# Input projection weights kept as split pairs in DRAM, and attention rows scaled on VectorE

## The chip, the cores and the metric

The kernel runs on one core of a Trainium2 chip. The metric is the device time of one execution in microseconds; the kernel before took 3005.1 us (median of 3 runs, 3004.28 to 3007.91). The profiled execution is one separate run.

## The reference

One decoder layer over 2048 tokens with 1024 features, all in fp32:

```
u = rmsnorm(h, attn_norm_g);  z = u @ w_in            # 1024 x 3592, the input projection
y_m = mLSTM of 4 heads from the columns (q, k, v, output gate, input and forget gate)
y_a = differential attention of 4 heads: two softmax maps of 64 dims per head, (A1 - lam A2) v
o   = rmsnorm(o, sub_g) * (1 - lam_init)               # per head and row, the end of y_a
h  += concat(y_m, y_a) @ w_out
h  += square(relu(rmsnorm(h) @ w_up)) @ w_down         # 1024 -> 4096 -> 1024
h  += sigmoid(rmsnorm(h) @ w_gate) * (p @ w_ple)
```

## The kernel before

**Split operands.** Every large product runs in a rounded fp32 type (F32R). To keep fp32 accuracy each operand x is split: hi is x rounded (a copy on ScalarE, line 75) and lo is x minus hi (a subtraction on GpSimd or VectorE, line 76). A product is three matmuls, hi·hi, hi·lo and lo·hi (`mm3`, lines 134 to 139).

**Two parts.** The first part (`phase1`) computes the input projection, mLSTM, attention and the first eighth of the output projection; the second (`phase2`, whose matmuls are line 923) the rest. The change is in the first part, which in the trace ends near 1290 us, where the first matmul of line 923 stands.

**Stages.** The tokens are cut into 4 tiles of 512, and the input projection's columns into 14 groups, 0 to 7 for mLSTM and 8 to 13 for attention. `ORDER` (line 37) gives eight stages: attention columns of tiles 0, 1, 2, mLSTM columns of tiles 0 and 1, attention of tile 3, mLSTM of tiles 2 and 3. Counted by the 192 matmuls of line 137 in each, the stages begin on TensorE at 6, 112, 243, 372, 525, 702, 839 and 1017 us, and the first out-projection at 1221 us. An attention stage uses 6 groups, an mLSTM stage 8, and each stage loads and splits its own weights, though other stages use the same ones for other tokens.

**Weights.** `load_w` (line 242) brings one group in four pieces of two 128-row blocks: SyncE issues a load into one of two `wraw` buffers (tile `rbuf` in the profile), ScalarE and GpSimd split it into one of eight hi and eight lo buffers (tile `wbuf`). `next_w` (line 265) calls it for the next group when the current one is about to be used, so loads run one group ahead. That makes 24 pieces in an attention stage, 32 in an mLSTM stage, 224 in all.

**Interleaving.** Attention units (one head, 128 query rows) run beside the projection. A loop in `phase1` (lines 575 to 593) picks the next piece of either by costs written in the code; mLSTM steps are woven in between. The order of instructions on each engine is then set at build time by a scheduler with its own timeline, so every engine works through a fixed list and waits at its head.

**Where the attention rows are scaled.** `attn_back` (line 815) sums the squares of the head's output on ScalarE (line 840), forms the argument on VectorE (841, 842), takes the power -1/2 on GpSimd (843) and multiplies the 128x128 tile by it on GpSimd (844). TensorE transposes the result (line 500) one unit later. The same pattern stands in `qk_prep` (line 723): a power on GpSimd (734), then products on VectorE (736).

**Queues.** All the DMAs of the kernel are issued by SyncE, in order, from one list.

Of the kernel before, what the change touches and what calls it, by code (L numbers as in the profile page):

```python
# [7 lines left out]
F32 = mybir.dt.float32  # L8
F32R = mybir.dt.float32r
BF16 = mybir.dt.bfloat16  # L10
AF = mybir.ActivationFunctionType
ALU = mybir.AluOpType
# [4 lines left out]
P = 128  # L17
D = 1024
S = 2048
KT = D // P  # L20
# [9 lines left out]
NW, NR, NKT, LEAD = 8, 2, 4, 4  # L30
# [10 lines left out]
def hybrid_block(ctx: ExitStack, tc: tile.TileContext, a: dict, out: bass.AP):  # L41
    nc = tc.nc

    const = ctx.enter_context(tc.tile_pool(name="const", bufs=1))
    dram = ctx.enter_context(tc.tile_pool(name="dram", bufs=1, space=DRAM))
# [7 lines left out]
    vdr = dram.tile([NH // 2, NT1, P, 4, 2 * P], F32, name="v_d")  # L53

# [40 lines left out]
    phase1(tc, a, wbuf, ubuf, rbuf, banks, yT, hd, qkdr, vdr, ident, identr, identb, masks, ones, negh, split, rstd_col, spread, acc0)  # L95
# [80 lines left out]
def phase1(tc, a, wbuf, ubuf, rbuf, ps, yT, hd, qkdr, vdr, ident, identr, identb, masks, ones, negh, split, rstd_col, spread, acc0):  # L176
    nc = tc.nc
    with ExitStack() as ctx:
# [7 lines left out]
        half = NW * 528  # L186
        for tag, base in (("whi", 0), ("wlo", half)):
            pw.put(tag, [cut(wbuf, base + i * 528, 2, 264) for i in range(NW)])
# [53 lines left out]
        def load_w(g, width, first=False):  # L242
            r = []
            for k in range(0, KT, 2):
                raw = pw.tile([P, 2, 264], F32, tag="wraw")[:, :, :width]
                hi = pw.tile([P, 2, 264], F32R, tag="whi")
                lo = pw.tile([P, 2, 264], F32R, tag="wlo")
                nc.sync.dma_start(raw, w_in[g, :, k:k + 2, :width])
                hi, lo = hi[:, :, :width], lo[:, :, :width]
                if first and k % 4 == 0:  # L250
                    nc.vector.tensor_copy(hi, raw)
                    nc.vector.tensor_tensor(out=lo, in0=raw, in1=hi.bitcast(F32), op=ALU.subtract)  # L252
                else:
                    split(raw, hi, lo)
                r += [(hi[:, i], lo[:, i]) for i in range(2)]
            return r

        wseq, wq = [], []
        for kind, j in ORDER:
            if kind == "a":  # L260
                wseq += [(8, 264)] + [(8 + g, 256) for g in range(1, 6)]
            else:
                wseq += [(g, 256) for g in (0, 1, 2, 3, 4, 5, 7, 6)]
# [551 lines left out]
def attn_back(nc, pa, ps, st, i, h, front, VV, ident, negh, out):  # L815
# [28 lines left out]
    nc.gpsimd.tensor_scalar(out=y, in0=y, scalar1=ss[:, 0:1], scalar2=None, op0=ALU.mult)  # L844
# [378 lines left out]
```

## Time and profile before

| | |
|---|---|
| median of 3 runs | 3005.1 us (3004.28 to 3007.91) |
| profiled execution | 2999.47 us, span 2997.7 us |
| mean granted TensorE clock | 0.988 of full speed |
| TensorE busy | 2872.7 us, 96% of the span |
| VectorE, ScalarE, GpSimd busy | 66%, 46%, 42% |
| DMA | 282.57 MB, 94 GB/s |

The page gives busy times over the whole span; the first part has other limits than the second, so it is read in windows. A window's PEclk is the mean clock that was granted, as a share of full speed. The durations of matmuls overlap, because they are pipelined. "Idle before" is the time an engine stood still before an instruction, with what released it.

### The profile page before, as it was taken

Reading aid. Unit: us, or ns where it says so; the run is one execution under the profiler, and the core shown is the slowest. Engines: PE = TensorE matmul, PEld = TensorE weight load, DVE = VectorE, ACT = ScalarE, POOL = GpSimd, SP = SyncE. Lnnn points to the kernel's source line nnn. Section 1 sums busy time; section 2 is a strip of 40 time slices with the busy share of each in tenths; the row PEclk is TensorE's granted clock in tenths of the full one; section 3 lists DMA queues with packets and bytes.
Section 4 is the critical chain, followed back from the end, with each engine's and each line's share of the span. In section 5 each row is a group of like instructions: output and inputs, shape, how many; then the busy total and the mean of one; then the engine's idle time right before and its main releaser. Section 6 shows DMA issues by size and latency. Waiting matters only on the chain.

```text
span 2997.7 us, 43151 instructions
## 1 busy us (share of the span) xinstructions
PE 2872.7 (96%) x15752; PEld 2460.7 (82%) x15752; DVE 1963.7 (66%) x3917; ACT 1377.7 (46%) x3134; POOL 1267.0 (42%) x980
## 2 busy tenths in 40 slices
PE   7798999899999899989999999999999999999999
PEld 7787988888988788867888888888878888888887
DVE  7788777767786766567555656564486555565653
ACT  4476766766666665544223332252342233322331
POOL 5666543434443332344333333362563333333441
PEclk9899999999999999999999999999999999999999
DMA  5654544334443423341111111124411111111211
GB/s 160 193 159 146 175 135 123 110 103 138 140 128 96 123 81 100 105 163 49 51 57 43 57 57 50 53 75 154 134 60 53 57 43 57 57 50 50 80 48 64
DMA packets 202421, 282.57 MB, mean 94 GB/s; under 512 B 16096, under 2 KB 143584, under 8 KB 198112
## 3 DMA queue, kind: packets, MB, share of 16 engines
q1 hardware_dynamic: 202208, 279.81, 30.7%
q8 instruction: 124, 2.03, 0.3%
q14 instruction: 89, 0.73, 0.1%
HBM read 239.90 MB, written 39.85 MB: 93 GB/s over the span
## 4 chain that ended last, share of the span: by engine, by line
PE 69%; DVE 14%; ACT 5%; DMA 4%; issue 4%; POOL 3%; SPq 0%; POOLq 0%; ACTq 0%; DVEq 0%
PE bank L923 52%; PE bank L137 3%; PE bank L138 3%; PE bank L139 3%; PE bank L834 2%; DMA rbuf<-in_w_in_dram 2%; DVE qn_r L736 2%; POOL wbuf L76 2%; DVE PP_r L810 2%; ACT PP_r L798 1%; DVE mxp_r L790 1%; PE bank L786 1%; PE bank L789 1%; PE bank L822 1%; POOL rn_r L734 1%
## 5 line engine op out<-in xcount | busy, mean ns | idle before, releaser
L76 POOL TENSOR_TENSOR wbuf<-rbuf,wbuf 128x512 fp32r<-128x512 f32 (+2 forms) x632 | 911.8, 1450 | 1321.8 <-ACT wbuf L75 1230.0
L75 ACT ACTIVATE wbuf<-rbuf 128x512 fp32r<-128x512 f32 (+2 forms) x632 | 415.1, 662 | 870.2 <-PE bank L923 600.7
L923 PE MATMUL bank<-U_r,wbuf 128*128 128x512 f32 x2928 | 701.1, 392 | 10.3 <-POOL wbuf L76 4.7
L923 PEld LDWEIGHTS bank<-U_r,wbuf 128*128 128x128 f32 x2928 | 551.1, 189 | 129.9 <-POOL wbuf L76 6.1
L923 PE MATMUL bank<-ubuf,wbuf 128*128 128x512 f32 x2208 | 574.7, 391 | 2.2 <-DVE ubuf L76 1.4
L888 DVE TENSOR_TENSOR h_r<-bank,h_r 128x512 f32<-128x512 f32 x504 | 343.3, 688 | 269.1 <-PE bank L923 267.5
L923 PEld LDWEIGHTS bank<-ubuf,wbuf 128*128 128x128 f32 x2208 | 414.8, 188 | 92.7 <-issue 2.9
L923 PE MATMUL bank<-ybuf,wbuf 128*128 128x512 f32 x1872 | 477.5, 390 | 5.4 <-ACT wbuf L75 4.6
L923 PEld LDWEIGHTS bank<-ybuf,wbuf 128*128 128x128 f32 x1872 | 351.3, 188 | 80.2 <-ACT wbuf L75 5.9
L137 PE MATMUL bank<-wbuf,ubuf 128*128 128x256 f32 (+1 forms) x1280 | 381.1, 298 | 25.0 <-ACT og_r L397 10.1
L138 PE MATMUL bank<-wbuf,ubuf 128*128 128x256 f32 (+1 forms) x1280 | 375.4, 293 | 0.9 <-DVE wbuf L252 0.9
L139 PE MATMUL bank<-wbuf,ubuf 128*128 128x256 f32 (+1 forms) x1280 | 373.6, 292 | 0.6 <-DVE ubuf L76 0.6
L137 PEld LDWEIGHTS bank<-wbuf,ubuf 128*128 128x128 f32 x1280 | 250.4, 196 | 34.1 <-ACT og_r L397 12.6
L138 PEld LDWEIGHTS bank<-wbuf,ubuf 128*128 128x128 f32 x1280 | 251.1, 196 | 3.9 <-DVE wbuf L252 1.5
L139 PEld LDWEIGHTS bank<-wbuf,ubuf 128*128 128x128 f32 x1280 | 250.5, 196 | 2.8 <-DVE ubuf L76 0.7
L790 DVE TENSOR_REDUCE mxp_r<-bank 128x1 f32<-128x512 f32 (+3 forms) x320 | 186.3, 603 | 68.6 <-PE bank L789 68.1
L798 ACT ACTIVATE PP_r<-bank,mx_r 128x512 f32<-128x512 f32 (+3 forms) x320 | 196.3, 622 | 53.8 <-DVE mx_r L795 47.4
L834 PE MATMUL bank<-V_r,at_r 128*128 128x128 f32 x1088 | 137.8, 279 | 0.9 <-ACT at_r L825 0.5
L786 PE MATMUL bank<-KT_r,QT_r 128*128 128x512 f32 (+3 forms) x320 | 124.7, 390 | 12.8 <-ACT PP_r L798 10.9
L834 PEld LDWEIGHTS bank<-V_r,at_r 128*128 128x128 f32 x1088 | 132.3, 196 | 3.4 <-ACT at_r L825 0.8
L137 PE MATMUL bank<-ubuf,wbuf 128*128 128x512 f32 x320 | 130.2, 407 | 2.4 <-DVE mx_r L794 1.2
L139 PE MATMUL bank<-ubuf,wbuf 128*128 128x512 f32 x320 | 127.8, 399 | 0.0
(285 smaller groups left out, 4244.8 us busy)
## 6 DMA issues: line engine op xcount, KB each, us to landing
rbuf<-in_w_in_dram SPq DMA_DIRECT2D x208, 256.0 KB, 2.8
rbuf<-in_w_down_dram SPq DMA_DIRECT2D x128, 256.0 KB, 2.6
rbuf<-in_w_up_dram SPq DMA_DIRECT2D x32, 1024.0 KB, 4.8
KT_r<-qk_d SPq DMA_DIRECT2D x40, 512.0 KB, 5.0
qk_d<-kst_r SPq DMA_DIRECT2D x64, 256.0 KB, 3.1
QT_r<-qk_d SPq DMA_DIRECT2D x128, 128.0 KB, 3.4
rbuf<-in_w_out_dram SPq DMA_DIRECT2D x32, 512.0 KB, 3.8
rbuf<-in_x_in_dram SPq DMA_DIRECT2D x31, 512.0 KB, 3.8
```

The lines of the kernel that those rows point to most:

```text
L75: nc.scalar.activation(hi, raw, AF.Copy)
L76: eng.tensor_tensor(out=lo, in0=raw, in1=hi.bitcast(F32), op=ALU.subtract)
L137: nc.tensor.matmul(ps, lhsT=lh, rhs=rh, start=(start and i == 0), stop=False)
L138: nc.tensor.matmul(ps, lhsT=lh, rhs=rl, start=False, stop=False)
L139: nc.tensor.matmul(ps, lhsT=ll, rhs=rh, start=False, stop=(stop and i == n - 1))
L736: nc.vector.scalar_tensor_tensor(out=qn[:, e], in0=qn[:, e], scalar=rn[:, e:e + 1], in1=qkg[:, e // 2], op0=ALU.mult, op1=ALU.mult)
L786: nc.tensor.matmul(Sp[:, 0:n], lhsT=QT[:, 0, m], rhs=rhs, start=True, stop=False)
L790: nc.vector.tensor_reduce(out=mxp[:, m, ci:ci + 1], in_=Sp[:, 0:n], op=ALU.max, axis=AX.X)
L798: nc.scalar.activation(pp[:, 0:n], sps[ci][:, 0:n], AF.Exp, bias=mx[:, m:m + 1], scale=0.125, accum_out=lp[:, m, ci:ci + 1])
L834: nc.tensor.matmul(po, lhsT=ats[kb // 4][:, (kb % 4) * P:(kb % 4 + 1) * P], rhs=VV[kb // 4][:, kb % 4], start=(kb == 0), stop=(kb == i))
L888: eng.tensor_tensor(out=out, in0=x, in1=y, op=op)
L923: nc.tensor.matmul(p, lhsT=l, rhs=r, start=start and i == q == 0, stop=stop and i == n - 1 and q == 2, skip_group_check=on)
```

## The change

Both parts of a split weight piece now lie side by side in one buffer `ws` (hi first, lo second). In the first stage that uses a group for keeping, the pieces are loaded and split as before, and each pair is then stored to a DRAM tensor `wsd`; the store is put into the program two pieces later. Attention groups 8 to 10 are kept in tile 1's stage (tile 0's stage splits them and does not store), groups 11 to 13 in tile 0's stage, mLSTM groups in tile 0's stage: 56 stores of 512 KB. In later stages the piece is one load of 512 KB from `wsd` straight into `ws`, without a split: 156 of the 224 pieces. In `attn_back` the multiplication of the tile moves from GpSimd to VectorE.

```
+    wsd = dram.tile([14, KT // 2, P, 4, 264], F32, name="ws_d")
...
-        half = NW * 528
-        for tag, base in (("whi", 0), ("wlo", half)):
-            pw.put(tag, [cut(wbuf, base + i * 528, 2, 264) for i in range(NW)])
+        pw.put("ws", [cut(wbuf, i * 1056, 2, 2, 264) for i in range(NW)])
...
+        kept, late_st = set(), []
+        flat4 = lambda t: t.bitcast(F32).rearrange("p a b c -> p (a b) c")
+        def store_w(lag):
+            while len(late_st) > lag:
+                ws, g, k, n = late_st.pop(0)
+                nc.sync.dma_start(wsd[g, k // 2, :, :, :n], flat4(ws)[:, :, :n])
-        def load_w(g, width, first=False):
+        def load_w(g, width, keep, first=False):
             r = []
             for k in range(0, KT, 2):
+                ws = pw.tile([P, 2, 2, 264], F32R, tag="ws")
+                hi, lo = ws[:, 0, :, :width], ws[:, 1, :, :width]
+                if g in kept:
+                    store_w(0)
+                    nc.sync.dma_start(flat4(ws)[:, :, :width], wsd[g, k // 2, :, :, :width])
+                    r += [(hi[:, i], lo[:, i]) for i in range(2)]
+                    continue
                 raw = pw.tile([P, 2, 264], F32, tag="wraw")[:, :, :width]
...
                     split(raw, hi, lo)
                 r += [(hi[:, i], lo[:, i]) for i in range(2)]
+                if keep:
+                    late_st.append((ws, g, k, width))
+                store_w(2)
+            if keep:
+                kept.add(g)
...
-                wseq += [(8, 264)] + [(8 + g, 256) for g in range(1, 6)]
+                wseq += [(8 + g, 256 if g else 264, j == (0 if g >= 3 else 1)) for g in range(6)]
             else:
-                wseq += [(g, 256) for g in (0, 1, 2, 3, 4, 5, 7, 6)]
+                wseq += [(g, 256, j == 0) for g in (0, 1, 2, 3, 4, 5, 7, 6)]
...
-    nc.gpsimd.tensor_scalar(out=y, in0=y, scalar1=ss[:, 0:1], scalar2=None, op0=ALU.mult)
+    nc.vector.tensor_scalar(out=y, in0=y, scalar1=ss[:, 0:1], scalar2=None, op0=ALU.mult)
```

In the order of instructions three places show it. The line numbers of the changed kernel are larger by 1 up to the head of `phase1`, and by 17 behind `load_w`.

GpSimd's list at the end of the last mLSTM stage, up to the first weights of the output projection (128x1024), before. Line 76 is the subtraction of a split, 706 and 843 are powers, 844 the scaling of an attention tile:

```order
L706 TENSOR_TENSOR mss_r<-mss_r,negh 128x4
L76 TENSOR_TENSOR wbuf<-rbuf,wbuf 128x2x256 x4
L843 TENSOR_TENSOR ass_r<-ass_r,negh 128x1
L844 TENSOR_SCALAR ya_r<-ya_r,ass_r 128x128
L76 TENSOR_TENSOR wbuf<-rbuf,wbuf 128x2x256 x4
L843 TENSOR_TENSOR ass_r<-ass_r,negh 128x1
L844 TENSOR_SCALAR ya_r<-ya_r,ass_r 128x128
L706 TENSOR_TENSOR mss_r<-mss_r,negh 128x4
L76 TENSOR_TENSOR wbuf<-rbuf,wbuf 128x2x256 x4
L843 TENSOR_TENSOR ass_r<-ass_r,negh 128x1
L844 TENSOR_SCALAR ya_r<-ya_r,ass_r 128x128
L76 TENSOR_TENSOR wbuf<-rbuf,wbuf 128x1024
```

The same place of GpSimd's list now (706 is 723, 843 is 860, 76 is 77):

```order
L723 TENSOR_TENSOR mss_r<-mss_r,negh 128x4
L860 TENSOR_TENSOR ass_r<-ass_r,negh 128x1 x2
L723 TENSOR_TENSOR mss_r<-mss_r,negh 128x4
L860 TENSOR_TENSOR ass_r<-ass_r,negh 128x1
L723 TENSOR_TENSOR mss_r<-mss_r,negh 128x4
L860 TENSOR_TENSOR ass_r<-ass_r,negh 128x1 x3
L723 TENSOR_TENSOR mss_r<-mss_r,negh 128x4
L77 TENSOR_TENSOR wbuf<-rbuf,wbuf 128x1024 x2
```

Only the powers are left; the splits of the weights and the scaling are gone from this stretch.

SyncE's list where the mLSTM columns of tile 1 end and the attention columns of tile 3 begin (128x528 is the first group), before. Line 248 loads a raw weight piece, 464, 441 keys and queries of attention, 719 stores an mLSTM result:

```order
L248 DMA rbuf<-in_w_in_dram 128x2x256 x4
L464 DMA KT_r<-qk_d 128x1024 x2
L248 DMA rbuf<-in_w_in_dram 128x2x256 x2
L441 DMA QT_r<-qk_d 64x2x256 x4
L248 DMA rbuf<-in_w_in_dram 128x2x256 x2
L464 DMA KT_r<-qk_d 128x1024
L719 DMA yT_d_74<-yo_r 128x512
L997 DMA pre<-yT_d_74 128x512
L248 DMA rbuf<-in_w_in_dram 128x2x256 x6
L248 DMA rbuf<-in_w_in_dram 128x528 x2
L441 DMA QT_r<-qk_d 64x2x256 x4
```

The same place now (257 loads a split pair, 481 and 458 are keys and queries, 736 is the store):

```order
L257 DMA wbuf<-ws_d 128x4x256 x4
L481 DMA KT_r<-qk_d 128x1024 x2
L458 DMA QT_r<-qk_d 64x2x256 x4
L481 DMA KT_r<-qk_d 128x1024
L736 DMA yT_d_74<-yo_r 128x512
L1014 DMA pre<-yT_d_74 128x512
L257 DMA wbuf<-ws_d 128x4x256 x8
L458 DMA QT_r<-qk_d 64x2x256 x4
L257 DMA wbuf<-ws_d 128x1056
```

A group's four loads now stand in one run, and each waits for TensorE to let go of its buffer instead of for the split of the raw buffer.

VectorE's list at one attention unit of the last mLSTM stage, now. Line 859 is before's 842, 861 the scaling that came from GpSimd's line 844:

```order
L859 SCALAR_TENSOR_TENSOR ass_r<-ass_r 128x1
L811 TENSOR_REDUCE mx_r<-mxp_r 128x1
L812 TENSOR_SCALAR mx_r<-mx_r 128x1
L712 SCALAR_TENSOR_TENSOR C_1_125<-C_1_125,g_ct_r,bank_72 128x129
L713 TENSOR_TENSOR N_r<-bank_72,I_r 128x129
L861 TENSOR_SCALAR ya_r<-ya_r,ass_r 128x128
L696 SCALAR_TENSOR_TENSOR Dm_r<-bank_73,Dm_r 128x128
```

Between 859 and 861, which waits for GpSimd's power of 859's result, four other instructions stand here; over the 64 units it is 0 to 16, and in 15 of them at most one.

## Rows read from the trace of the kernel before

**Rows 1.** Section 1 of the page: engine, busy us, share, instructions.
```profile
PE 2872.7 (96%) x15752; PEld 2460.7 (82%) x15752; DVE 1963.7 (66%) x3917; ACT 1377.7 (46%) x3134; POOL 1267.0 (42%) x980
```

**Rows 2.** Busy time by stage: window, length, engines with instruction counts, clock, DMA share, GB/s.
```profile
core 0: us, PE busy (x) PEld busy (x) DVE busy (x) ACT busy (x) POOL busy (x), PEclk, DMA share, GB/s
0.00:112.00 112.00, 87.45 (x646) 83.13 (x647) 83.17 (x247) 51.36 (x96) 63.87 (x56) 0.98 0.60 172
112.00:166.00 54.00, 43.46 (x296) 40.13 (x295) 44.96 (x157) 28.51 (x72) 35.34 (x36) 0.85 0.55 166
166.00:355.00 189.00, 173.45 (x1360) 161.46 (x1359) 156.35 (x535) 129.67 (x366) 113.24 (x112) 0.98 0.54 157
355.00:502.00 147.00, 143.41 (x989) 128.64 (x989) 116.59 (x301) 99.17 (x279) 69.62 (x59) 1.00 0.47 139
502.00:702.00 200.00, 189.33 (x1323) 171.36 (x1322) 147.41 (x355) 137.79 (x394) 80.28 (x68) 0.99 0.39 115
702.00:839.00 137.00, 126.99 (x993) 119.61 (x992) 101.23 (x309) 92.16 (x247) 66.44 (x63) 0.98 0.49 145
839.00:1017.00 178.00, 169.83 (x1125) 149.86 (x1124) 135.07 (x303) 116.52 (x323) 67.71 (x54) 0.98 0.35 103
1017.00:1221.00 204.00, 189.94 (x1285) 168.69 (x1286) 134.54 (x327) 130.15 (x375) 57.47 (x50) 0.98 0.33 96
```

**Rows 3.** Chain of waits by line: 166:355, then 702:839, then 1017:1221.
```profile
by line: DVE qn_r L736 10.7%; issue 9.6%; DVE mxp_r L790 5.4%; POOL wbuf L76 5.2%; PE bank L137 4.5%; PE bank L138 4.4%; POOL rn_r L734 4.4%; PE bank L139 4.3%; DVE PP_r L810 4.2%; PE bank L834 3.4%; ACT PP_r L798 3.4%; DVE KS_r L751 2.8%; 
...
by line: issue 16.7%; DVE qn_r L736 9.6%; POOL rn_r L734 9.2%; POOL wbuf L76 8.3%; DMA rbuf<-in_w_in_dram 7.2%; DVE mxp_r L790 3.4%; ACT PP_r L798 2.9%; ACT wbuf L75 2.5%; DMA pre<-yT_d 2.5%; DVE PP_r L810 2.0%; DMA QT_r<-qk_d 2.0%; PE bank
...
by line: issue 14.7%; PE bank L137 8.3%; PE bank L834 8.1%; PE bank L138 7.8%; PE bank L139 7.7%; DMA rbuf<-in_w_in_dram 7.5%; PE bank L786 4.1%; ACT PP_r L798 3.9%; PE bank L789 3.7%; PE bank L822 3.4%; DVE mxp_r L790 2.7%; POOL wbuf L76 2
```

**Rows 4.** Waits of 0:1330: engine and line, waited for; total us, times, longest.
```profile
ACT wbuf L75 <- DMA rbuf<-in_w_in_dram: 94.3, 63, 5.3
...
DVE qn_r L736 <- POOL rn_r L734: 14.2, 19, 1.9
```

**Rows 5.** Timeline of ScalarE from 1122 to 1134: start, duration, instruction, idle before.
```profile
1131.36 0.63 ACT L75 ACTIVATE wbuf<-rbuf 128x512 fp32r<-128x512 f32 x1 [3.46 <-DMA rbuf<-in_w_in_dram]
...
1133.01 0.36 ACT L397 ACTIVATE og_r<-bank,rcol 128x128 f32<-128x128 f32 x1
```

**Rows 6.** Timeline of TensorE from 1126 to 1134, the same columns.
```profile
1133.42 0.39 PE L137 MATMUL bank<-wbuf,ubuf 128*128 128x256 f32 x1 [3.58 <-ACT og_r L397]
```

**Rows 7.** Groups by line and form, 0:1330, of GpSimd, ScalarE, VectorE.
```profile
L76 POOL TENSOR_TENSOR wbuf<-rbuf,wbuf 128x512 fp32r<-128x512 f32 x208 | 281.5, 1363 | 307.3 <-ACT wbuf L75 289.9 <-PE bank L789 4.5 <-PE bank L138 3.8
...
L844 POOL TENSOR_SCALAR ya_r<-ya_r,ass_r 128x128 f32<-128x128 f32 x64 | 47.2, 737 | 5.3
L843 POOL TENSOR_TENSOR ass_r<-ass_r,negh 128x1 f32<-128x1 f32 x64 | 39.6, 618 | 153.0 <-DVE ass_r L842 130.3 <-DVE mx_r L794 11.8 <-ACT Dm_r L678 7.5
...
L75 ACT ACTIVATE wbuf<-rbuf 128x512 fp32r<-128x512 f32 x208 | 129.9, 635 | 95.8 <-DMA rbuf<-in_w_in_dram 82.3 <-PE bank L139 5.5 <-PE bank L138 5.0
...
L736 DVE SCALAR_TENSOR_TENSOR qn_r<-qn_r,rn_r,qkg 128x64 f32<-128x64 f32 x256 | 92.0, 415 | 14.7 <-POOL rn_r L734 14.2
...
L90 DVE TENSOR_SCALAR row_r<-ident,rcol 128x128 f32<-128x128 f32 x16 | 5.7, 399 | 0.0
```

**Rows 8.** Timeline of VectorE, then GpSimd, from 220 to 245.
```profile
226.01 1.67 DVE L736 SCALAR_TENSOR_TENSOR qn_r<-qn_r,rn_r,qkg 128x64 f32<-128x64 f32 x2
...
232.12 0.87 DVE L736 SCALAR_TENSOR_TENSOR qn_r<-qn_r,rn_r,qkg 128x64 f32<-128x64 f32 x4
...
225.94 1.31 POOL L76 TENSOR_TENSOR wbuf<-rbuf,wbuf 128x528 fp32r<-128x528 f32 x1
```

**Rows 9.** DMA queue of the page, then DMA issues of 0:1330 with landing time.
```profile
q1 hardware_dynamic: 202208, 279.81, 30.7%
...
rbuf<-in_w_in_dram SPq DMA_DIRECT2D x208, 256.0 KB, 2.8
KT_r<-qk_d SPq DMA_DIRECT2D x40, 512.0 KB, 5.0
```

More of the change, by code (lines that the diff above doesn't have):

```diff
@@ L93, in spread @@
         nc.vector.tensor_copy(out_t, pb)
-    phase1(tc, a, wbuf, ubuf, rbuf, banks, yT, hd, qkdr, vdr, ident, identr, identb, masks, ones, negh, split, rstd_col, spread, acc0)
+    phase1(tc, a, wbuf, ubuf, rbuf, banks, yT, hd, qkdr, vdr, wsd, ident, identr, identb, masks, ones, negh, split, rstd_col, spread, acc0)
     phase2(tc, a, wbuf, ubuf, rbuf, ybuf, pre, acc0, g23, banks, yT, hd, out, split, rstd_col, spread)
@@ L173, in tile, with phase1 @@
         return cut(t[0:shape[0]], 0, *shape[1:], cast=None if dtype == F32 else dtype)
-def phase1(tc, a, wbuf, ubuf, rbuf, ps, yT, hd, qkdr, vdr, ident, identr, identb, masks, ones, negh, split, rstd_col, spread, acc0):
+def phase1(tc, a, wbuf, ubuf, rbuf, ps, yT, hd, qkdr, vdr, wsd, ident, identr, identb, masks, ones, negh, split, rstd_col, spread, acc0):
     nc = tc.nc
@@ L240, in phase1 @@
         pl = lambda t: t.rearrange("p a b -> p (a b)")
-        def load_w(g, width, first=False):
+        kept, late_st = set(), []
[5 more added lines that the diff above has]
+        def load_w(g, width, keep, first=False):
             r = []
             for k in range(0, KT, 2):
+                ws = pw.tile([P, 2, 2, 264], F32R, tag="ws")
[5 more added lines that the diff above has]
+                    continue
                 raw = pw.tile([P, 2, 264], F32, tag="wraw")[:, :, :width]
-                hi = pw.tile([P, 2, 264], F32R, tag="whi")
-                lo = pw.tile([P, 2, 264], F32R, tag="wlo")
                 nc.sync.dma_start(raw, w_in[g, :, k:k + 2, :width])
-                hi, lo = hi[:, :, :width], lo[:, :, :width]
                 if first and k % 4 == 0:
```

## The prediction

> **What bounds the kernel now.** I read section 1 of the page first. TensorE is busy for 2872.7 of 2997.7 us [rows 1], so with the same 15752 matmuls only its idle time and its slow clock can be won. Then I read the busy times by stage, since the change touches the first part alone. The windows of [rows 2] are cut where the change cuts: pieces are still split until about 166 us (the third group of tile 1, one group ahead of its use) and again, with stores, from 355 to 502 us (mLSTM of tile 0). From 166 to 355 and from 502 to 1221 us every piece would be loaded ready. Call these five windows the loaded stages; they last 908 us.
>
> In the loaded stages TensorE is idle for 15.6, 10.7, 10.0, 8.2 and 14.1 us, window less busy time, 58.5 us in all. The clock column adds what the half-rate stretches cost: (1 - clock) times the length gives 3.8, 2.0, 2.7, 3.6 and 4.1, together 16.2 us [rows 2]. The ceiling is their sum, 74.7 us, on the reading that idle time is all there is to win. VectorE is the next busiest, 675 us of the 908 (74%), and 83% in the first of these windows.
>
> What ends TensorE's waits is seen in the chain of waits. In three of the five windows it gives shares for the work that goes: subtraction 5.2% of 189 us, 9.8 us; subtraction 8.3, raw load 7.2 and copy 2.5% of 137 us, 24.7 us; raw load 7.5% of 204 us, 15.3 us [rows 3]. That is 50 us of chain. The mechanism is plain in one place: ScalarE stood still for 3.46 us at the head of its list for a raw piece that had not landed, the eviction of the gate (L397) stood behind it, and TensorE then waited 3.58 us for that eviction [rows 5, 6]. ScalarE waited so 63 times, for 94.3 us [rows 4], though most of these waits have no TensorE gap behind them.
>
> **What the change removes.** Each of 156 pieces loses a copy of 635 ns on ScalarE and a subtraction of 1363 ns on GpSimd [rows 7]: 99 us and 213 us of engine time, none of it TensorE's. VectorE gains as well. Two products of L736 that met a subtraction of 1.31 us took 1.67 us, and four that met none took 0.87 us [rows 8], so the pair lost about 1.2 us.
>
> The Trainium skill (SBUF — State Buffer, "SBUF: two separate sides") says that GpSimd and a VectorE instruction with two SBUF inputs share a pair of ports under an exclusive lock, and that the loser stands still for the whole instruction. The rows agree: the 1.2 us lost is nearly the whole 1.31 us. By that rule 156 removed subtractions could free up to 156 x 1.36 = 212 us of VectorE, an estimate that needs a VectorE instruction to meet each one; it is the third rival below.
>
> What this is worth on TensorE is bounded from both sides. Nothing is the lower end, since the engines that get lighter are not the busiest one, and the window from 355 to 502 us, with the same splits, idles for only 3.6 us [rows 2]. A loss from this part alone I exclude, since no work is put in the place of the copies. The upper end is the ceiling of 74.7 us. I take half, 37 us: the 50 us of chain are not all direct, because the next chain (the attention maxima and exponentials, also in [rows 3]) is close behind, and they cover three windows of five.
>
> **What it adds: stores.** 56 stores of 512 KB are 29 MB, and 156 loads grow by 256 KB, 41 MB. The queue moved 279.81 MB in 30.7% of its time [rows 9], so at full share it would move 304 GB/s. The stores are then 97 us and the larger loads 135 us of full share. From 355 to 502 us, 32 stores (16.8 MB) add 55 us, so the share goes from 0.47 to 0.85. From 112 to 166 us 12 stores (6.3 MB, 21 us) take it from 0.55 to 0.93. The last third of the first window gets as many. A raw piece lands 2.8 us after issue, and a 512 KB load of keys, the nearest row to a crowded queue, 5.0 us [rows 9]. If 24 raw pieces in the first two stages came 2.2 us later, with two buffers in flight, that is 26 us. The lower end is 0, since pieces are fetched a group ahead; a gain I exclude, as nothing there becomes lighter. I take 10 us, nearer to 0, since the first two stages alone wait visibly for their loads. From 355 to 502 us I take nothing: the eight groups of that stage use some 18 us each and four pieces through two buffers at 5.0 + 0.6 + 1.4 us need 14. If that cover goes, each of the eight groups is 2 to 4 us late, 16 to 32 us.
>
> **What it adds: larger loads.** A loaded group is 2 MB, 6.9 us at full share, or 20 us if four loads of 5.0 us followed one another. TensorE needs 204/8 = 25 us for a group in the last stage and 189/9 = 21 us in the first loaded one, and the loads run a group ahead. So I take nothing between a lower end of 0 (a gain from earlier data is in the 37 us already) and an upper end given by the second rival. The 56 further issues are no bound on SyncE.
>
> **What it moves: the scaling of an attention tile.** GpSimd loses 64 x 737 ns = 47 us, VectorE gets 64 times an instruction of up to 399 ns, the mean of the nearest row (L90, the same shape), 26 us [rows 7]. The added wait is for the power on GpSimd, 618 ns by its row. Behind the scaling on VectorE stand the maxima of the next scores, for which ScalarE's exponentials wait. The order puts 0 to 16 instructions between argument and scaling and at most one in 15 units, so 15 x 0.6 = 9 us of VectorE wait. The like wait of L736 for its power was 14.2 us over 64 tiles, even with subtractions in front of it [rows 4]. 26 + 14 = 40 us is less than the two-input products alone get back if one in five of the 156 subtractions cost VectorE 1.2 us (37 us), near enough to even. I take 0, with bounds of 10 us faster (transposes start earlier) and 10 us slower (a quarter of the 40 us reaches TensorE).
>
> **The sum.** 2999.5 us of the profiled execution (2997.7 us of span and 1.8 around it) - 37 + 10 + 0 + 0 = 2972.5. The median of the runs is 5.6 us above the profiled execution, so I forecast 2978 us, 27 below 3005.
>
> **Rivals.**
>
> 1. The splits are hidden anyway. For it: most waits of ScalarE for raw pieces leave no gap, and the window from 355 to 502 us is the tightest of all with its splits. Against it: 50 us of chain. If a quarter of the half comes (9 us) and the stores take 10, the time is 3006.
>
> 2. Slower: the keys come late. A group's four loads stand in one run on SyncE, each waiting for TensorE to let go of a buffer, and queries and keys stand behind them. About 12 of the 16 head starts lie in the loaded stages. A start whose keys are queued behind a full group is 6.9 us late, and with half of that covered by projection matmuls 12 x 3.5 = 42 us are lost. For it: the list shows such runs of four and eight loads. Against it: the raw loads waited in the same way for GpSimd, and GpSimd for TensorE. The time is 2978 + 42 = 3020. It decides if a key load takes over 8 us, or TensorE waits for keys for more than 30 us in all; under 10 us it plays no part. The Trainium skill (HBM Reference, "Latency") gives 0.2 us for an access on average and 2 us at high load; no run here shows it, and by it alone each start would be 1.8 us later, 22 us in all.
>
> 3. More: VectorE is freed as the lock lets it, the attention chain shrinks by more than it takes to keep ahead of TensorE, and the whole ceiling comes. For it: 83% of VectorE in the first loaded window, and the pair in [rows 8]. Against it: some gaps follow matmuls that TensorE's own list puts too close, which stay. 2999.5 - 74.7 + 10 + 5.6 = 2940.
>
> **Chances.** The forecast has 0.54, with a range of its own from 2960 to 2994. Rival 1 has 0.18, rival 2 0.16, rival 3 0.12. The measurement tells about 0.2%, 6 us, from no change. Faster is the forecast, rival 3 and a quarter of rival 1: 0.70. Within 0.2% is most of the rest of rival 1: 0.13. Slower is rival 2 and a little of rival 1: 0.17. The range runs from the whole ceiling, 2938, to 3012, where rival 2 is half paid.
>
> **What would show it.** Right: in the loaded stages no ScalarE wait for raw pieces, 66 instead of 222 subtractions of weights up to 1221 us (two of the 224 are done on VectorE), L736 well under 415 ns, and idle plus clock loss near 38 instead of 75 us. The stores' term: the idle time up to 166 us grows from 35 us to about 45, and the share from 355 to 502 us goes to about 0.85. The scaling: a wait of VectorE for L860 of under 20 us. Wrong: idle time in the loaded stages that stays above 50 us, with the attention chain alone behind it (rival 1), or TensorE waiting for keys (rival 2).

## The result and the profile after

The changed kernel takes 2961.8 us (median of 4 runs, 2959.96 to 2963.7) where the kernel before took 3006.3 us in the runs beside it (4 runs): a ratio of 0.985 [0.9839, 0.9862], 44 us faster. The profiled execution took 2959.96 us, 39.5 us less than the one before.

All of it lies in the first part. The first matmul of the second part (its line 923, now 940, in the form that reads the attention rows) starts at 1241.45 us instead of 1284.93, 43.5 us earlier; from there to the end of the span it is 1716.7 us instead of 1712.8, 4 us more.

Section 1 of the page of after, which answers to [rows 1]: engine, busy us, share, instructions.

```profile
PE 2868.3 (97%) x15752; PEld 2464.4 (83%) x15752; DVE 1889.4 (64%) x3981; ACT 1301.6 (44%) x2978; POOL 1007.4 (34%) x760
```

TensorE's matmuls are the same 15752. ScalarE has 156 copies less, and GpSimd 156 subtractions and 64 scalings. VectorE has 64 instructions more and is busy for 74 us less: its instructions have become shorter.

The windows of after, cut at nearly the same points of the work as [rows 2] (the counts of matmuls tell), with the columns of that group. The first two and the fourth have splits and stores; the third and the last four are the loaded stages.

```profile
core 0: us, PE busy (x) PEld busy (x) DVE busy (x) ACT busy (x) POOL busy (x), PEclk, DMA share, GB/s
0.00:105.00 105.00, 86.76 (x645) 83.38 (x646) 82.67 (x245) 48.72 (x91) 58.47 (x52) 0.97 0.78 237
105.00:164.00 59.00, 48.77 (x318) 44.63 (x317) 54.34 (x181) 33.55 (x90) 41.21 (x39) 0.83 0.85 265
164.00:334.00 170.00, 165.29 (x1334) 157.59 (x1334) 127.08 (x535) 107.64 (x311) 52.10 (x55) 0.98 0.77 232
334.00:485.00 151.00, 145.81 (x990) 130.95 (x990) 113.10 (x306) 98.94 (x278) 56.33 (x49) 0.98 0.81 252
485.00:684.00 199.00, 191.26 (x1331) 171.80 (x1330) 134.46 (x368) 122.08 (x366) 26.14 (x24) 0.99 0.52 159
684.00:809.00 125.00, 121.55 (x967) 116.24 (x966) 92.02 (x317) 81.64 (x220) 33.04 (x34) 0.97 0.68 208
809.00:992.00 183.00, 175.50 (x1193) 156.37 (x1191) 123.55 (x322) 102.80 (x302) 16.16 (x14) 0.99 0.53 163
992.00:1175.00 183.00, 177.92 (x1224) 159.16 (x1223) 115.00 (x314) 109.06 (x324) 17.05 (x15) 0.99 0.44 137
```

The five loaded stages last 170, 199, 125, 183 and 183 us, 860 in all, where they were 908: 48 us less for nearly the same matmuls (6049 in the windows, 6086 before). TensorE idles in them for 4.7, 7.7, 3.5, 7.5 and 5.1 us, 28.5 instead of 58.5, and the clock loss is 12.8 instead of 16.2: the two together fall from 74.7 to 41.3 us. The rest of the first part is 4.5 us longer in sum: up to 164 us it is 2 us shorter, the stage from 334 to 485 us 4 us longer (151 for 147), and the stretch from 1175 us to the end of the part 2.5 us longer.

The chain of waits of after in two of these stages, 684 to 809 and 992 to 1175 us, answers to the last two lines of [rows 3].

```profile
by line: PE bank L140 17.9%; PE bank L139 17.6%; PE bank L138 17.6%; PE bank L851 9.3%; PE bank L806 4.8%; PE bank L839 4.8%; PE bank L803 4.5%; DVE mxp_r L807 2.9%; PE bank L775 2.8%; DVE rbuf L315 2.7%; PE bank L692 1.3%; ACT PP_r L815 1.
...
by line: PE bank L138 16.5%; PE bank L140 15.7%; PE bank L139 15.5%; PE bank L851 10.9%; PE bank L803 6.0%; PE bank L806 5.9%; PE bank L839 5.4%; DMA KT_r<-qk_d 2.7%; PE bank L692 2.3%; PE bank L705 2.1%; PE bank L702 1.9%; PE bank L704 1.8
```

Before, "issue" stood at the head of both lines, followed by the product of L736, powers, subtractions and raw loads in the first and by matmuls and raw loads in the second; now TensorE's own matmuls lead both. In the second a load of keys stands with 2.7% of 183 us, 4.9 us: the only sign, in what these two lines show, of the queue that got fuller.

The waits of after up to 1290 us, which answer to [rows 4]: engine and line, waited for; total us, times, longest.

```profile
ACT wbuf L76 <- DMA rbuf<-in_w_in_dram: 27.8, 17, 4.8
...
DVE qn_r L753 <- POOL rn_r L751: 8.3, 17, 1.1
DVE ya_r L861 <- POOL ass_r L860: 6.4, 13, 0.7
...
PE bank L803 <- DMA KT_r<-qk_d: 3.0, 1, 3.0
```

ScalarE waits 27.8 us for raw pieces instead of 94.3, all of it in stages that still split. TensorE waits for keys once.

Groups by line and form of after up to 1290 us, answering to [rows 7]: instructions, then busy us and mean ns of one, then idle before and its releasers.

```profile
L77 POOL TENSOR_TENSOR wbuf<-rbuf,wbuf 128x512 fp32r<-128x512 f32 x60 | 81.2, 1355 | 85.1 <-ACT wbuf L76 78.6 <-DMA rbuf<-in_w_in_dram 2.8 <-PE bank L140 2.3
L753 DVE SCALAR_TENSOR_TENSOR qn_r<-qn_r,rn_r,qkg 128x64 f32<-128x64 f32 x256 | 70.9, 331 | 8.6 <-POOL rn_r L751 8.3
...
L861 DVE TENSOR_SCALAR ya_r<-ya_r,ass_r 128x128 f32<-128x128 f32 x64 | 20.7, 323 | 6.8 <-POOL ass_r L860 6.4
...
L77 POOL TENSOR_TENSOR wbuf<-rbuf,wbuf 128x528 fp32r<-128x528 f32 x6 | 10.3, 1724 | 11.4 <-ACT wbuf L76 11.4
```

The same 256 products of two SBUF operands take 331 ns each instead of 415, 21 us less in sum, and 60 + 6 subtractions of weights are left.

The DMA issues of after up to 1290 us, answering to [rows 9]: size of one and median us from issue to landing.

```profile
wbuf<-ws_d SPq DMA_DIRECT2D x148, 512.0 KB, 5.5
ws_d<-wbuf SPq DMA_DIRECT2D x52, 512.0 KB, 5.1
KT_r<-qk_d SPq DMA_DIRECT2D x40, 512.0 KB, 6.5
...
rbuf<-in_w_in_dram SPq DMA_DIRECT2D x60, 256.0 KB, 3.9
```

Keys land after 6.5 us instead of 5.0. The 3.9 us of the raw pieces should not be set against the 2.8 of [rows 9], which is the median over all stages, while the 60 that are left lie in the crowded ones. Stage against stage the medians are 3.8 us for 3.4 (up to 164 and 166 us) and 4.0 for 2.7 (the mLSTM columns of tile 0).

### The profile page after: what moved, and what is told of

The parts are those of the page before. It is cut to its first block, busy times and chain, and to the rows that moved or that the text cites. A ratio compares the mean times of both kernels' runs of the same rounds, so it can differ in the third digit from the quotient of the medians.

```text
span 2958.2 us, 42725 instructions
## 1 busy us (share of the span) xinstructions
PE 2868.3 (97%) x15752; PEld 2464.4 (83%) x15752; DVE 1889.4 (64%) x3981; ACT 1301.6 (44%) x2978; POOL 1007.4 (34%) x760
## 4 chain that ended last, share of the span: by engine, by line
PE 83%; DVE 10%; DMA 3%; ACT 3%; issue 1%; POOL 1%; SPq 0%; ACTq 0%; DVEq 0%; POOLq 0%
PE bank L940 51%; PE bank L138 6%; PE bank L140 6%; PE bank L139 6%; PE bank L851 4%; PE bank L806 2%; PE bank L803 2%; PE bank L839 2%; DVE qn_r L753 1%; DVE U_r L77 1%; DMA rbuf<-in_x_in_dram 1%; DVE mxp_r L807 1%; ACT PP_r L815 1%; DVE rbuf L315 1%; DVE rbuf L905 1%
## 5 line engine op out<-in xcount | busy, mean ns | idle before, releaser
L77 POOL TENSOR_TENSOR wbuf<-rbuf,wbuf 128x512 fp32r<-128x512 f32 (+2 forms) x476 | 699.9, 1475 | 1086.2 <-ACT wbuf L76 1021.4
L940 PE MATMUL bank<-U_r,wbuf 128*128 128x512 f32 x2928 | 699.5, 391 | 12.5 <-ACT wbuf L76 5.6
L76 ACT ACTIVATE wbuf<-rbuf 128x512 fp32r<-128x512 f32 (+2 forms) x476 | 317.8, 670 | 812.7 <-PE bank L940 586.5
L940 PE MATMUL bank<-ubuf,wbuf 128*128 128x512 f32 x2208 | 577.2, 392 | 4.6 <-DVE ubuf L77 2.8
L138 PE MATMUL bank<-wbuf,ubuf 128*128 128x256 f32 (+1 forms) x1280 | 379.7, 297 | 12.5 <-ACT ubuf L299 5.7
L815 ACT ACTIVATE PP_r<-bank,mx_r 128x512 f32<-128x512 f32 (+3 forms) x320 | 196.4, 623 | 65.0 <-DVE mx_r L812 52.7
L860 POOL TENSOR_TENSOR ass_r<-ass_r,negh 128x1 f32<-128x1 f32 x64 | 40.1, 626 | 477.6 <-DVE ass_r L859 442.1
L138 PE MATMUL bank<-ubuf,wbuf 128*128 128x512 f32 x320 | 129.6, 405 | 1.0 <-DVE rbuf L557 1.0
```

Of the source, the lines that this page charges most:

```text
L76: nc.scalar.activation(hi, raw, AF.Copy)
L77: eng.tensor_tensor(out=lo, in0=raw, in1=hi.bitcast(F32), op=ALU.subtract)
L138: nc.tensor.matmul(ps, lhsT=lh, rhs=rh, start=(start and i == 0), stop=False)
L815: nc.scalar.activation(pp[:, 0:n], sps[ci][:, 0:n], AF.Exp, bias=mx[:, m:m + 1], scale=0.125, accum_out=lp[:, m, ci:ci + 1])
L940: nc.tensor.matmul(p, lhsT=l, rhs=r, start=start and i == q == 0, stop=stop and i == n - 1 and q == 2, skip_group_check=on)
```

## The experiments

The question was which of the things removed pays. Four causes were on the table: GpSimd's subtractions hold the ports that VectorE needs; ScalarE's (and behind it GpSimd's) list stands still for raw pieces that have not landed; ScalarE's copies take time; or the change only deals a luckier order. Ratios are to runs of the kernel before on the same chip, and every kernel gets an order of its own from the scheduler. Line numbers move a little between the kernels (the product of L753 is L756 or L754 below).

**1. The weights alone** (after, with the scaling back on GpSimd) **and 2. the scaling alone** (before, with the scaling on VectorE).

```
-    nc.vector.tensor_scalar(out=y, in0=y, scalar1=ss[:, 0:1], scalar2=None, op0=ALU.mult)     # 1, in after
+    nc.gpsimd.tensor_scalar(out=y, in0=y, scalar1=ss[:, 0:1], scalar2=None, op0=ALU.mult)
...
-    nc.gpsimd.tensor_scalar(out=y, in0=y, scalar1=ss[:, 0:1], scalar2=None, op0=ALU.mult)     # 2, in before
+    nc.vector.tensor_scalar(out=y, in0=y, scalar1=ss[:, 0:1], scalar2=None, op0=ALU.mult)
```

> The weights are kept as split pairs in DRAM as in the change, but the attention tiles are still scaled on GpSimd. Theory A (ScalarE's and GpSimd's lists are freed of the splits, and TensorE's gaps behind them go): nearly all of the gain is here, 2960 to 2970 us. Rival B (the scaling on VectorE brings a good part, since TensorE's transposes wait for it): 2975 to 2990 us. Rival C (the gain is mostly the luck of another order of instructions): anything between 2960 and 3005, without a relation to the splits.

> Only the scaling of the attention tiles moves to VectorE; every stage still splits its weights. Theory A: 2999 to 3009 us, no change that can be told, or slightly slower, since VectorE now waits for powers that stand behind subtractions in GpSimd's list. Rival B: 2975 to 2992 us. Rival C: as far from 3005 as the change is, in either direction.

Measured: the weights alone 2958.2 us, 0.9836 [0.9821, 0.9851]; the scaling alone 3005.6 us, 0.9992 [0.9983, 1.0002]. So the weights bring all of the gain and the scaling none: theory A, with the weights alone a little under its range. Each of the two kernels agrees with its neighbour to within the intervals. After, the kernel of experiment 1 and, below, those of experiments 6, 8, 9 and 11 are six kernels that load the split pairs, each in an order of its own, and all lie between 2958 and 2968 us. So the luck of an order is not the cause of 44 us. In the kernel with the scaling alone the products still take 414 ns:

```profile
L736 DVE SCALAR_TENSOR_TENSOR qn_r<-qn_r,rn_r,qkg 128x64 f32<-128x64 f32 x256 | 92.2, 414 | 11.2 <-POOL rn_r L734 10.8
```

It is the subtractions, not the 64 scalings, that had lengthened them.

**3. The subtraction back and 4. the copy back.** In after, each loaded piece is followed by work as long as the one that went, on the engine that it went from. It reads the piece of the same number of the group before (`po`) and writes a free raw buffer; its result is used by nothing.

```
+                po, old[k] = old.get(k), ws
...
                     nc.sync.dma_start(flat4(ws)[:, :, :width], wsd[g, k // 2, :, :, :width])
+                    x = pw.tile([P, 2, 264], F32, tag="wraw")[:, :, :256]
+                    nc.gpsimd.tensor_tensor(out=x, in0=po[:, 0, :, :256].bitcast(F32), in1=po[:, 1, :, :256].bitcast(F32), op=ALU.subtract)   # 3
+                    nc.scalar.activation(x, po[:, 0, :, :256].bitcast(F32), AF.Copy)                                                          # 4
```

> As the change, but for each of the 156 loaded pieces GpSimd does a subtraction of the same size on the piece of the group before, which has long landed, into an unused buffer: GpSimd gets its time back and VectorE its rival for the ports, and nobody waits for the result but later powers in GpSimd's list. If the freed ports are what paid (VectorE's products met by subtractions), half or more of the gain goes: 2980 to 3000 us, and L753's mean rises from 331 to about 400 ns. If it was ScalarE's list and the waits for raw pieces, 2960 to 2970 us.

> As the change, but for each of the 156 loaded pieces ScalarE makes a copy of the same size from the piece of the group before, which has long landed: ScalarE's 99 us come back, without a wait for a load. If ScalarE's time paid: 2975 to 2990 us. If it was the waits of ScalarE for raw pieces or GpSimd's ports: 2960 to 2968 us.

Measured: with the subtraction 3025.5 us, 1.0059 [1.0043, 1.0074], slower than before; with the copy 2991.1 us, 0.9938 [0.9921, 0.9954]. The first lies above both of its ranges and the second just above the one for ScalarE's time. Both expected a piece that "has long landed", which the traces do not show. Groups of the first kernel up to 1310 us, then of the second:

```profile
L260 POOL TENSOR_TENSOR rbuf<-wbuf 128x512 f32<-128x512 f32 x156 | 216.5, 1392 | 281.5 <-DMA wbuf<-ws_d 279.5
L756 DVE SCALAR_TENSOR_TENSOR qn_r<-qn_r,rn_r,qkg 128x64 f32<-128x64 f32 x256 | 89.3, 404 | 20.5 <-POOL rn_r L754 20.3
...
L864 DVE TENSOR_SCALAR ya_r<-ya_r,ass_r 128x128 f32<-128x128 f32 x64 | 23.1, 361 | 17.1 <-POOL ass_r L863 17.0
```

```profile
L260 ACT ACTIVATE rbuf<-wbuf 128x512 f32<-128x512 f32 x156 | 98.3, 633 | 110.9 <-DMA wbuf<-ws_d 108.7 <-POOL wbuf L77 1.4
```

The added work stands at the head of its list until a load has landed, 279.5 us in all on GpSimd and 108.7 us on ScalarE. On GpSimd the powers stand behind it: VectorE waits 20.3 and 17.0 us for them, instead of 8.3 and 6.4 in after. So each of the two runs holds two costs at least, the work and a wait (and the buffer that is read can't be loaded anew before that). The next runs part them.

**5. The subtraction early, 6. a memset early, and 9. the copy early.** The same work for the same 156 pieces, now before the load, in the buffer that the load then overwrites. It needs no data; like the load it waits until TensorE lets the buffer go, and the load waits for it.

```
+                    nc.gpsimd.tensor_tensor(out=lo, in0=hi.bitcast(F32), in1=lo.bitcast(F32), op=ALU.subtract)   # 5
+                    nc.gpsimd.memset(ws[:, :, :, :width].bitcast(F32), 0.0)                                      # 6
+                    nc.scalar.activation(hi, lo.bitcast(F32), AF.Copy)                                           # 9
                     nc.sync.dma_start(flat4(ws)[:, :, :width], wsd[g, k // 2, :, :, :width])
```

> As the change, but before each of the 156 loads of a split pair GpSimd does a subtraction of the same size inside the buffer that the load will overwrite. It waits for TensorE to let go of the buffer, as the splits before did, and for no load. If GpSimd's 213 us on the shared ports are what paid: 2985 to 3010 us, VectorE's L753 back at about 400 ns. If it was the waits in GpSimd's list for data that had not landed (279.5 us in the run with the subtraction put back): 2962 to 2975 us.

> The same place, but GpSimd only fills the buffer with zeros (a memset over both halves, no SBUF operand is read) before the load overwrites it. If the ports matter as a lock against instructions that read SBUF: VectorE's L753 stays near 331 ns and the time near the change, 2962 to 2972 us. If it is GpSimd's list being occupied: as the subtraction in the same place, scaled by the durations.

> As the change, but before each of the 156 loads ScalarE makes a copy of the same size inside the buffer that the load will overwrite; it waits for TensorE to let go of the buffer and for no load. The copy put back on landed pieces cost 29 us with 109 us of waits for loads. If ScalarE's 99 us of time cost TensorE something by themselves: 2975 to 2990 us. If only the waits did: 2960 to 2970 us.

Measured: with the subtraction 2997.8 us, 0.997 [0.9956, 0.9984]; with the memset 2960.5 us, 0.9849 [0.9832, 0.9866]; with the copy 2960.8 us, 0.9839 [0.9824, 0.9854]. The first is in the range for the ports, the second a little under its range for a lock against reads, the third in the range for "only the waits". Groups of the kernel with the subtraction, then of those with the memset and with the copy:

```profile
L257 POOL TENSOR_TENSOR wbuf<-wbuf 128x512 fp32r<-128x512 f32 x148 | 201.0, 1375 | 215.1 <-PE bank L140 165.1 <-PE bank L139 24.1 <-issue 20.4
L754 DVE SCALAR_TENSOR_TENSOR qn_r<-qn_r,rn_r,qkg 128x64 f32<-128x64 f32 x256 | 93.0, 418 | 9.9 <-POOL rn_r L752 9.2
```

```profile
L257 POOL MEMSET wbuf<- 128x1024 f32 x148 | 138.6, 954 | 263.2 <-issue 181.2 <-PE bank L140 77.0 <-POOL wbuf L257 3.8
L754 DVE SCALAR_TENSOR_TENSOR qn_r<-qn_r,rn_r,qkg 128x64 f32<-128x64 f32 x256 | 68.3, 325 | 11.6 <-POOL rn_r L752 11.1
L862 DVE TENSOR_SCALAR ya_r<-ya_r,ass_r 128x128 f32<-128x128 f32 x64 | 33.2, 518 | 5.9 <-POOL ass_r L861 5.2
```

```profile
L257 ACT ACTIVATE wbuf<-wbuf 128x512 fp32r<-128x512 f32 x148 | 91.8, 642 | 12.4 <-PE bank L139 6.4 <-PE bank L140 4.6 <-DMA KT_r<-qk_d 0.2
```

And the window of the whole first part, with the columns of [rows 2]: first after, then the subtraction, then the memset.

```profile
0.00:1241.00 1241.00, 1176.91 (x8350) 1073.56 (x8351) 869.60 (x2646) 738.71 (x2065) 321.87 (x291) 0.98 0.62 191
```

```profile
0.00:1282.00 1282.00, 1187.17 (x8321) 1078.13 (x8322) 958.18 (x2645) 735.78 (x2062) 533.98 (x447) 0.97 0.61 185
```

```profile
0.00:1245.00 1245.00, 1173.99 (x8350) 1070.14 (x8351) 879.49 (x2644) 735.01 (x2063) 467.56 (x446) 0.98 0.62 191
```

The subtraction gives back 36 of the 44 us (2997.8 against 2961.8), with no wait for a load in it. With as good as the same number of instructions VectorE is busy for 89 us more (958.2 against 869.6), 0.57 us for each of the 156 subtractions, and the product is back at 418 ns.

Which instructions grow is telling. Here are two more groups, of after and then of the kernel with the subtraction: a sum with two inputs in SBUF (the convolution before mLSTM), and the maxima of the scores, whose one input lies in PSUM (`bank`).

```profile
L430 DVE SCALAR_TENSOR_TENSOR cv_r<-zc_r,cw,cv_r 128x512 f32<-128x512 f32 x96 | 76.7, 799 | 8.1 <-ACT cv_r L428 7.8
L807 DVE TENSOR_REDUCE mxp_r<-bank 128x1 f32<-128x512 f32 x224 | 150.5, 684 | 88.6 <-PE bank L806 88.1
```

```profile
L431 DVE SCALAR_TENSOR_TENSOR cv_r<-zc_r,cw,cv_r 128x512 f32<-128x512 f32 x96 | 91.4, 952 | 8.7 <-ACT cv_r L429 8.0
L808 DVE TENSOR_REDUCE mxp_r<-bank 128x1 f32<-128x512 f32 x224 | 151.4, 684 | 48.9 <-PE bank L807 48.2
```

The sum goes from 799 to 952 ns (781 with the memset), the maxima stay at 684. And the lengthened product stands in the chain of waits. Before, it had 10.7% of the first loaded stage [rows 3]; here are the chains of that stage in after (164 to 334 us) and with the subtraction (164 to 347 us):

```profile
by line: PE bank L138 20.3%; PE bank L140 19.6%; PE bank L139 19.6%; PE bank L851 8.6%; PE bank L806 5.7%; PE bank L803 5.6%; PE bank L775 3.9%; PE bank L839 3.7%; DVE qn_r L753 2.2%; DVE rbuf L315 2.2%; PE bank L805 1.3%; DVE mxp_r L807 1.
...
by line: PE bank L138 13.0%; PE bank L139 12.7%; PE bank L140 12.5%; DVE qn_r L754 10.1%; PE bank L852 7.0%; PE bank L807 4.9%; PE bank L804 4.4%; PE bank L840 3.5%; PE bank L776 3.3%; issue 2.3%; POOL rn_r L752 1.7%; DVE mxp_r L808 1.7%; D
```

The memset stands at the same point of the program, and the load waits for it too. It costs nothing and leaves the product at 325 ns. The waits of VectorE for powers, 9.2 and 11.1 us, do not tell the two apart. Besides the order two differences are left: the subtraction reads SBUF, and it takes longer, so GpSimd is occupied for 213 us (201.0 and 11.8 of the wider form) against 146 (138.6 and 7.8). ScalarE's copy, 642 ns each and 97 us in all, costs nothing where it waits for no load. That leaves the waits for landings as the likeliest cause of the 29 us of experiment 4.

The Trainium skill (SBUF — State Buffer, "SBUF: two separate sides") makes just this distinction: a VectorE instruction with two SBUF inputs contends only with a GpSimd instruction that reads SBUF, while one in a mode that uses both port pairs contends with any. The first half agrees with 418 against 325 ns. The scaling, with one tile as input, takes 518 ns beside the memsets and 323 in after; that would fit the second half, but no run here shows in which mode it runs.

**7. Four raw buffers in before, and 8. the same in the kernel with the weights alone.** Two more buffers for raw pieces of 256 columns, cut from tiles that the first part leaves free.

```
+        pw.put("wraw256", [cut(rbuf, 3072 + i * 528, 2, 256) for i in range(NR)] + [cut(pre, 0, 2, 256), cut(acc0, 0, 2, 256)])
...
-                raw = pw.tile([P, 2, 264], F32, tag="wraw")[:, :, :width]
+                raw = pw.tile([P, 2, 264], F32, tag="wraw256" if width == 256 else "wraw")[:, :, :width]
```

> The kernel before with four raw weight buffers instead of two for the 256-wide groups (two more lie in tiles that the first part uses late), so that a group's four loads are issued together and land earlier; every split stays. If ScalarE's waits for raw pieces (94.3 us) were a good part of what the change removed: 2980 to 2995 us. If it was the engine time of the splits: 3000 to 3010 us.

> Split pairs in DRAM, scaling on GpSimd, and four raw buffers for the pieces that are still split. If the splits that remain (tile 0 and 1's first groups) still lose time to late raw pieces (41.6 us of ScalarE waits in the run without them): 2945 to 2955 us. If they lose nothing on TensorE: 2955 to 2963 us.

Measured: in before 2995.9 us, 0.9969 [0.9958, 0.998]; with the weights 2961.2 us, 0.985 [0.9835, 0.9865]. The waits of ScalarE for raw pieces in the first kernel, up to 1310 us (the second line is one of the new buffers):

```profile
ACT wbuf L75 <- DMA rbuf<-in_w_in_dram: 7.1, 4, 4.1
ACT wbuf L75 <- DMA acc<-in_w_in_dram: 2.6, 1, 2.6
```

94.3 us of waiting become some 10 [rows 4], with all splits in place, and the time falls by 0.31%, 9 us, 1 us outside the range for the waits. That is about what the late raw pieces were worth. Once the loaded pieces are there, nothing of it is left to win (the second range).

**10. Every store issued twice**, the second time into another DRAM tensor that nothing reads.

```
                 nc.sync.dma_start(wsd[g, k // 2, :, :, :n], flat4(ws)[:, :, :n])
+                nc.sync.dma_start(wsd2[g, k // 2, :, :, :n], flat4(ws)[:, :, :n])
```

> As the change, but each of the 56 stores is issued a second time into another DRAM tensor: 29 MB more, in tile 0 and 1's attention stages and tile 0's mLSTM stage, where the DMA share is already high. If the stores cost what was forecast for them (10 us or more): 2970 to 2985 us. If they lie beside other work: 2958 to 2967 us.

Measured: 2984.3 us, 0.992 [0.9903, 0.9936], 22 us slower than after and thus in the range for a cost of 10 us or more. Windows of the first four stretches; they are cut some 10 us later than in after, and still at less work (2172 matmuls by 345 us, 2297 by 334 us in after):

```profile
0.00:117.00 117.00, 90.32 (x659) 84.84 (x659) 81.53 (x256) 49.30 (x96) 55.79 (x50) 0.97 0.83 252
117.00:175.00 58.00, 39.80 (x226) 34.44 (x227) 48.41 (x161) 29.05 (x83) 30.13 (x31) 0.79 0.98 316
175.00:345.00 170.00, 161.86 (x1287) 153.74 (x1286) 123.67 (x501) 103.34 (x288) 60.25 (x59) 0.96 0.83 253
345.00:495.00 150.00, 145.73 (x1044) 132.32 (x1043) 113.49 (x322) 99.03 (x281) 53.78 (x47) 1.00 0.99 308
```

The first set of stores took the share to 0.85 and 0.81 and cost little; the second takes it to 0.98 and 0.99, and from 117 to 175 us TensorE idles for 18.2 of 58 us, against 10.2 of 59 in after. At the 6.9 matmuls per us of after, the 125 missing ones and the 11 us make some 29 us lost by 345 us. The fourth window is as full and loses nothing like that (1044 matmuls in 150 us, 990 in 151 in after), although raw pieces land after 5.9 us there, and after 4.1 up to 175 us. Nor is it in the main loads that TensorE waits for from 117 to 175 us. 10.6 of the 18.2 us are waits for ScalarE's exponentials (L818), and these wait for VectorE's maxima (L815):

```profile
ACT PP_r L818 <- DVE mx_r L815: 11.6, 5, 7.0
PE bank L806 <- ACT PP_r L818: 10.6, 5, 4.8
```

So the second set is no measure of the first, and the run does not show by what path it costs 22 us; a full queue alone does not explain it.

**11. The remaining subtractions of the weights on VectorE** (in the kernel with the weights alone) **and 12. all of them, in before**, without any copy in DRAM.

```
-                    split(raw, hi, lo)
+                    split(raw, hi, lo, nc.vector)
```

> Split pairs in DRAM, attention tiles scaled on GpSimd, and the subtractions of the 68 pieces that are still split moved from GpSimd (1.39 us each) to VectorE (0.69 us for this shape by another line). If a subtraction on GpSimd costs VectorE more through the ports than doing it itself: 2945 to 2956 us, better than the change. If VectorE's own time is what bounds those stages: 2960 to 2975 us.

> The kernel before with all the weight subtractions on VectorE; nothing is kept in DRAM. VectorE gets about 222 x 0.69 = 153 us and loses the roughly 100 us by which subtractions on GpSimd lengthen its products. If the ports were the whole cost of GpSimd's subtractions: 3000 to 3015 us, about as before. If GpSimd's list (its powers behind subtractions) mattered beyond the ports: 2975 to 2995 us.

Measured: the former 2967.6 us, 0.986 [0.9845, 0.9874], not faster than after and in its second range; the latter 2985.2 us, 0.9919 [0.9903, 0.9936], in its second range too. Groups of the latter up to 1310 us, and then its window of the first part, behind which stands that of before:

```profile
L76 DVE TENSOR_TENSOR wbuf<-rbuf,wbuf 128x512 fp32r<-128x512 f32 x208 | 141.7, 688 | 59.3 <-ACT wbuf L75 57.2 <-PE bank L789 1.3
L736 DVE SCALAR_TENSOR_TENSOR qn_r<-qn_r,rn_r,qkg 128x64 f32<-128x64 f32 x256 | 66.3, 315 | 6.0 <-POOL rn_r L734 6.0
```

```profile
0.00:1269.00 1269.00, 1182.93 (x8352) 1073.56 (x8353) 939.23 (x2804) 819.12 (x2223) 297.43 (x289) 0.98 0.45 132
```

```profile
0.00:1285.00 1285.00, 1184.66 (x8352) 1073.46 (x8353) 944.32 (x2581) 815.86 (x2221) 579.53 (x509) 0.98 0.44 130
```

With 222 subtractions more on its list, 151 us of them (141.7 and another 9.7 of the wider form), VectorE is busy for 939 us where it was for 944: what it took over it gets back in shorter instructions (the product 315 ns for 415). The kernel is 0.8% faster by one word, with ScalarE still waiting 90.9 us for raw pieces. So VectorE's busy time in sum is not what sets the pace. By the expectation the rest is GpSimd's list, and the waits for powers do fall (6.0 us for 14.2 [rows 4]); but the instructions that TensorE waits for have become shorter as well, and no run parts the two. The Trainium skill (GPSIMD Engine Reference, "3.1 Elementwise — side-by-side cycle accounting") puts a two-input operation of 2048 fp32 at 4497 ns on GpSimd and 2293 on VectorE; the rows here, 1363 and 688 ns for 512, have the same ratio of two.

None of the versions beats the change by more than the intervals: 0.9836 and 0.985 for the weights alone with two or four raw buffers, 0.986 with the rest on VectorE.

## Why the prediction was right, and where not

The forecast was 2978 us, 27 below before; it is 2961.8, 44 below: inside the range and near the lower end of the likeliest case's own. The side, the place and the signs were right, and two terms of the sum were mis-sized.

- **The splits, -37: too small.** The loaded stages became 48 us shorter. The half of the ceiling that was taken came out of idle time and clock almost as forecast: 74.7 became 41.3, where 38 was expected. That half was a choice and much of what paid was another mechanism (next point), so the closeness is in part luck. What failed is the step "on the reading that idle time is all there is to win". TensorE's busy time in these stages fell too, by 18 us (849.5 to 831.5): some 5 are 37 matmuls fewer in the windows, 3 are the smaller clock loss. Some of the other 10 comes from where the windows are cut, for over the whole first part, with the same matmuls, idle time falls by 36 us (100.3 to 64.1) and busy time by 8.
- **What pays in this term: mostly another mechanism.** Its working put direct subtractions, raw loads and copies on the chain, and called the 213 us of GpSimd "none of it TensorE's". By experiment 5 the subtractions alone carry 36 of 44 us, and VectorE's 89 us change with them; by experiment 7 the late raw pieces carry 9 in before; by experiment 9 the copies nothing. 36 and 9 make up the whole, though the two need not add. That VectorE would gain was said, from two instructions in [rows 8], but as a side effect and as rival 3. [rows 3] showed more: the product stood there with 10.7 and 9.6% of two stages, some 20 and 13 us, and was left out of the 50 us of chain. So did [rows 7]: at the 218 ns of the four products in [rows 8], the 256 would take 56 us instead of the 92 they were busy for.
- **The reading of [rows 8].** The four products did not meet no subtraction: one ran from 232.72 to 234.18 us and began before the last of them had ended (232.99). What followed is the better case for the lock. The instruction behind the four, on one column with two inputs in SBUF and with a median of 142 ns, took 1.29 us and ended with the subtraction:

```profile
232.72 1.46 POOL L76 TENSOR_TENSOR wbuf<-rbuf,wbuf 128x528 fp32r<-128x528 f32 x1 [1.27 <-ACT wbuf L75]
...
232.90 1.29 DVE L841 SCALAR_TENSOR_TENSOR ass_r<-ll_r 128x1 f32<-128x1 f32 x1
```

- **The stores, +10: too large.** The idle time up to 164 us did not grow from 35 to 45; it is 28.5 us, and that stretch is 2 us shorter. In the stage from 334 to 485 us, where nothing was taken, it is 4 us longer. The share came out about as worked out there (0.81 for 0.85) and below it from 105 to 164 us (0.85 for 0.93), and in the first two stages raw pieces landed 0.4 us later, not 2.2. The net of +2 is not the price of the stores alone, since no run loads the pairs without storing them. -37 for -48 and +10 for about +2 are 19 us, against the 16 by which the forecast was too high; the stretch behind 1175 us, 2.5 us longer, is most of the difference.
- **Larger loads, 0: right.** TensorE waits 3.0 us for keys, once; keys land after 6.5 us, under the 8 us from which rival 2 was to decide. By the prediction's own bound (under 10 us) rival 2 plays no part.
- **The scaling, 0: right.** With the scaling on VectorE, after is 0.1% slower than the kernel of experiment 1, and that of experiment 2 is 0.1% faster than before; neither is clear of the intervals. VectorE waits 6.4 us for the power (under 20), and the instruction takes 323 ns instead of the 399 of the nearest row.
- **Rival 1, hidden anyway: wrong.** The window that spoke for it, with its splits and 3.6 us of idle time, does not show that splits are free: experiments 5 and 12 show their price. Why it idles so little is open.
- **Rival 3, the lock: right in mechanism, as far as experiments 5 and 6 show it, not in size.** Its 2940 needs the whole 74.7 us, and 41.3 of these stayed. Its counter-argument, gaps that TensorE's own list makes, was not tested.
- **Slips that change nothing.** 40 us is not "less than" 37, and rival 2 half paid is 2999 us, not 3012, which lies half way from 3005 to 3020.

What stays open: how much of the 28 us between experiments 3 and 5 is GpSimd's list standing in front of the powers (VectorE's waits for them are 21 us longer in experiment 3), since no run has the wait alone; whether the memset is free because it reads nothing or in part because it is a third shorter; how much of the gain of experiment 12 is GpSimd's list; and why moving the last 66 subtractions to VectorE brings nothing where moving 222 in before brought 0.8%.

## What to carry to other kernels

An engine that is far from busy can still set the pace by lengthening another engine's instructions: compare one instruction's duration beside its neighbour's work and without it, over all its instances, before calling removed work hidden. Here busy time of an in-order engine cost less than work that stands at its list's head until a load has landed: 97 us of copies were free in one place and went with 29 us in another. Spare queue share was cheap here at 0.85; the same bytes again cost 22 us, by a path that the runs do not show.

## What the runs showed of the hardware

- 156 GpSimd subtractions of some 1.4 us lengthened VectorE's work by 89 us in sum: the two groups with two inputs in SBUF that are shown grew (331 to 418 and 799 to 952 ns), the one that reads PSUM did not (684). 156 memsets of 954 ns lengthened it by 10 us; the one scaling of 128x128 alone grew by 12.5.
- A 128x512 subtraction of the split takes 1363 ns on GpSimd [rows 7] and 688 on VectorE, which for 222 of them ended up no busier for doing them itself.
- In the stage of tile 0's mLSTM columns the median landing of a raw piece of 256 KB went from 2.7 us (before) to 4.0 (after) and 5.9 (stores twice), while the share went from 0.47 to 0.81 and 0.99.
